# Forward scan of a hybrid trunk: output factors loaded one chunk ahead, through a ring of seven

## The chip, the cores and the metric

One kernel on one core of a Trainium2 chip. The metric is device time in microseconds of the whole launch; the median of the timed runs stands for a kernel. Engines: PE multiplies matrices (PEld is its weight load), DVE is the vector engine, ACT the scalar engine with its function tables, POOL the third elementwise engine, SP the queue from which nearly all transfers are issued.

## What is computed

Two layers, each with a normalised input, one input projection, four mixers and one output projection. The change lies in one mixer, a state-space scan that runs over the sequence in both directions in chunks. For one direction:

```python
cs = jnp.cumsum(da, axis=-1)                          # da = dt * a, per head
lmat = jnp.exp(jnp.where(lower, cs[..., :, None] - cs[..., None, :], -jnp.inf))
y_diag = einsum(cb[:, :, :, None] * lmat, xdt)        # inside a chunk
chunk_states = einsum(bc, exp(cs[..., -1:] - cs), xdt)
h = h * exp(cs[..., -1]) + chunk_states               # from chunk to chunk
y_off = einsum(cc, prev, jnp.exp(cs))                 # from the chunks before
y = y_fwd + y_bwd + d_skip * xh
y = rmsnorm(y * silu(z), norm_w)
```

`exp(cs)`, by which `y_off` is multiplied, is what the text calls the output factors.

## The kernel before

The sequence has 1040 positions, channels lie on partitions. Filler work, the output projections of the other mixers (`outproj`, three matmul passes, lines 132 to 134, 12 matmuls for one output tile, scalar copy L349 and POOL addition L350 or DVE addition L352 behind it), is woven into the scan by `weave`. The order in which the code is written gives priorities; a scheduler then fixes an order for each engine and gives each tile a free slot of its pool. Every engine works through its own order and waits where a row is not ready.

The backward scan `ssd_bwd` leaves one state for each chunk. The forward scan `ssd_fwd` goes over ten chunks of 104 positions (q = 0 to 9) in two parts:

- `prepare(q)` loads two copies of the cumulative sums, `rf` and `rb`, broadcast over the partitions, from `csd` (L865, L866), transposes the chunk (`ssd_tok`), and makes the decay matrix: eight times DVE L880 and ACT L881 on `rf`, masks L877 and L878, eight times ACT L884 and DVE L885 into `rb`, and one POOL product L886 of the two. `rf` is free after L886, `rb` after the matmuls L911.
- `finish(q, st)` loads the output factors `e` from `ecd` with two transfers (L894), multiplies the parts that come from the backward state (matmul L822, DVE L897) and from the forward state (L822, DVE L900) by them, makes the new state (`ssd_state`: DVE L805, matmul L808, POOL L814, DVE L815), adds the two parts on POOL (L905), runs the matmuls inside the chunk (L911), adds them (DVE L912) and writes four tiles of `y` (DVE L914).

The matmul L808 writes the accumulator tile that L900 reads, so L808 waits for L900. Where an output part of `CH` is complete (after chunks 3, 6 and 9), `ssd_fin` gates it with z (ACT table load and SiLU at L306, DVE L947), squares it (ACT L949, DVE L951), and in a second half sums over partitions (matmul L954), takes the reciprocal root (`rstd`: ACT L138 Ln, L140 Exp, L142, DVE L143 to L145) and scales (DVE L958). SiLU is in another table of ACT than Ln and Exp; L307 asks for the table that has both of these.

`rf` and `rb` come from the pool `bb`, which has 5 slots of 8 x 104 floats; `e` comes from the common pool `big`. The order of the parts is prepare 0, prepare 1, finish 0, prepare 2, finish 1, and so on; the second half of a norm is written behind the prepare that follows its first half.

## Time and profile before

| | us |
|---|---|
| median of 3 runs (lowest, highest) | 2119.06 (2115.15, 2121.02) |
| profiled execution | 2122.54 |
| its span in the trace | 2120.80 |
| PE, DVE, ACT, POOL busy | 1995.3, 1396.7, 1012.3, 461.1 |
| first and last L897 of layer 0 | 914.2, 1038.4 |
| first and last L897 of layer 1 | 1955.5, 2070.9 |

The profiled execution is 3.48 us above the median and 1.52 us above the slowest of the three runs; 1.74 us of it lie around its span. The trace gives, for each instruction, start, duration and, in brackets, how long its engine stood idle before it and on whom it waited. A group line gives the count, the busy time with the mean in ns, and the idle time before the group. Start times are microseconds from the start of the span.

### The profile page before, as it was taken

The page shows a single profiled execution, that of the slowest core. Times are in us where ns is not written, and L with a number is a line of the kernel's source. Part 1 is how long each engine was busy: PE and PEld are TensorE (multiplying, and loading weights), DVE is VectorE, ACT ScalarE, POOL GpSimd, SP SyncE. Part 2 cuts the span into 40 slices and gives each one's busy share as a digit, 9 for nine tenths or more (in the row PEclk, how much of TensorE's full clock was granted, in tenths as well). Part 3 has the DMA queues.
Part 4 walks back from the last instruction along what each step waited for, and adds up shares of the span by engine and source line. Part 5 has one row for each costly group of instructions (what it writes and reads, how often), then busy time and mean ns, then how long its engine had stood idle before and what let it go on. Part 6 is the DMA issues. An engine that isn't in the chain of part 4 may idle for free.

```text
span 2120.8 us, 33393 instructions
## 1 busy us (share of the span) xinstructions
PE 1995.3 (94%) x11880; PEld 1747.7 (82%) x11880; DVE 1396.7 (66%) x2781; ACT 1012.3 (48%) x2191; POOL 461.1 (22%) x465
## 2 busy tenths in 40 slices
PE   6999999999999998888899999999999999989888
PEld 4898988688899778877779988877888996878878
DVE  5575547767665555689786755477676636476996
ACT  5534344463543546356465343436534425563652
POOL 2012122022120300245220121221311203012550
PEclk8999999999999999999999999999999999999999
DMA  4321222122232567676643221122223335867766
GB/s 139 100 75 60 67 64 57 42 74 97 92 125 97 171 196 249 188 184 187 172 130 112 75 67 54 58 61 69 71 89 104 119 112 169 243 215 183 185 176 194
DMA packets 164669, 261.01 MB, mean 123 GB/s; under 512 B 20938, under 2 KB 113678, under 8 KB 164502
## 3 DMA queue, kind: packets, MB, share of 16 engines
q1 hardware_dynamic: 161846, 249.56, 39.3%
q0 software_dynamic: 2656, 9.33, 1.8%
q8 instruction: 93, 1.52, 0.3%
q14 instruction: 74, 0.61, 0.1%
HBM read 182.92 MB, written 71.67 MB: 120 GB/s over the span
## 4 chain that ended last, share of the span: by engine, by line
PE 66%; DVE 12%; DMA 10%; ACT 5%; issue 4%; POOL 3%; SPq 1%; DVEq 0%; POOLq 0%; ACTq 0%
PE psmm L132 10%; PE psmm L133 10%; PE psmm L134 10%; PE pspv L675 6%; PE psy L132 5%; PE psy L133 5%; PE psy L134 5%; PE psy L652 2%; PE psy L623 2%; DMA hd<-sms 2%; PE psy L653 2%; DMA big<-md 2%; DMA sms<-hd 2%; DMA sms<-md 1%; PE pssc L652 1%
## 5 line engine op out<-in xcount | busy, mean ns | idle before, releaser
L132 PE MATMUL psmm<-big,wh 128*128 128x346 f32 (+2 forms) x1920 | 643.5, 336 | 29.3 <-ACT sms L349 10.3
L133 PE MATMUL psmm<-big,wh 128*128 128x346 f32 (+2 forms) x1920 | 632.3, 329 | 6.0 <-DVE big L129 3.2
L134 PE MATMUL psmm<-big,wl 128*128 128x346 f32 (+2 forms) x1920 | 626.1, 326 | 1.3 <-DVE wl L129 1.3
L132 PEld LDWEIGHTS psmm<-big,wh 128*128 128x128 f32 x1920 | 369.6, 193 | 74.7 <-issue 29.2
L133 PEld LDWEIGHTS psmm<-big,wh 128*128 128x128 f32 x1920 | 369.3, 192 | 15.6 <-DVE big L129 5.4
L134 PEld LDWEIGHTS psmm<-big,wl 128*128 128x128 f32 x1920 | 369.2, 192 | 4.7 <-DVE wl L129 2.4
L665 POOL TENSOR_TENSOR acc<-acc,pf 116x346 f32<-116x346 f32 (+5 forms) x216 | 220.8, 1035 | 673.4 <-ACT pf L655 534.0
L128 ACT CAST wh<-wr 128x512 fp32r<-128x512 f32 (+1 forms) x236 | 145.1, 616 | 264.1 <-PE psmm L133 207.3
L129 DVE TENSOR_TENSOR wl<-wr,wh 128x512 fp32r<-128x512 f32 x232 | 170.1, 737 | 126.6 <-ACT wh L128 125.3
L132 PE MATMUL psy<-big,wh 128*128 128x346 f32 (+2 forms) x672 | 221.6, 330 | 1.0 <-ACT big L128 0.4
L133 PE MATMUL psy<-big,wh 128*128 128x346 f32 (+2 forms) x672 | 217.5, 324 | 2.6 <-DVE big L188 1.5
L134 PE MATMUL psy<-big,wl 128*128 128x346 f32 (+2 forms) x672 | 216.6, 322 | 0.0
L655 ACT ACTIVATE pf<-psy 116x346 f32<-116x346 f32 (+4 forms) x288 | 125.1, 456 | 90.2 <-PE psy L653 89.0
L675 PE MATMUL pspv<-pf,vt 116*64 116x346 f32 (+5 forms) x864 | 166.0, 465 | 0.0
L665 DVE TENSOR_TENSOR acc<-acc,pf 116x346 f32<-116x346 f32 (+5 forms) x120 | 108.8, 907 | 77.1 <-ACT pf L655 50.8
L624 DVE TENSOR_REDUCE mx<-psy 116x1 f32<-116x346 f32 (+3 forms) x272 | 132.8, 511 | 17.6 <-PE psy L623 17.1
L132 PEld LDWEIGHTS psy<-big,wh 128*128 128x128 f32 x672 | 126.9, 189 | 12.9 <-issue 7.4
L133 PEld LDWEIGHTS psy<-big,wh 128*128 128x128 f32 x672 | 126.8, 189 | 6.0 <-DVE big L188 2.3
L134 PEld LDWEIGHTS psy<-big,wl 128*128 128x128 f32 x672 | 127.0, 189 | 0.8
L675 PEld LDWEIGHTS pspv<-pf,vt 116*64 116x64 f32 (+1 forms) x864 | 59.0, 136 | 61.6 <-issue 25.8
L624 DVE TENSOR_REDUCE mx<-pssc 128x1 f32<-128x346 f32 (+3 forms) x136 | 69.9, 514 | 41.4 <-PE pssc L623 39.8
L652 PE MATMUL psy<-big,big 128*116 128x346 f32 (+4 forms) x288 | 95.5, 333 | 1.0 <-DVE mx L624 0.9
(292 smaller groups left out, 3310.7 us busy)
## 6 DMA issues: line engine op xcount, KB each, us to landing
wr<-w SPq DMA_DIRECT2D x248, 256.0 KB
sms<-hd SPq DMA_DIRECT2D x112, 173.0 KB
hd<-sms SPq DMA_DIRECT2D x96, 173.0 KB
bb<-csd SPq DMA_DIRECT2D x40, 338.0 KB
md<-big SPq DMA_DIRECT2D x24, 520.0 KB
gd<-sms SPq DMA_DIRECT2D x64, 173.0 KB
big<-gd SPq DMA_DIRECT2D x16, 520.0 KB
big<-md SPq DMA_DIRECT2D x16, 520.0 KB
```

What stands on the lines that cost most here:

```text
L128: nc.scalar.copy(hi, src)
L129: nc.vector.tensor_tensor(lo, src, f(hi), op=ALU.subtract)
L132: nc.tensor.matmul(out_ps, ah, bh, start=start, stop=False)
L133: nc.tensor.matmul(out_ps, ah, bl, start=False, stop=False)
L134: nc.tensor.matmul(out_ps, al, bh, start=False, stop=stop)
L623: nc.tensor.matmul(p[:qn, :cw], s1[e][:, q0:q0 + qn], k1[:, c0:c0 + cw], start=True, stop=True)
L624: nc.vector.tensor_reduce(mx[:qn, q, e, ci:ci + 1], p[:qn, :cw], axis=AX.X, op=ALU.max)
L652: nc.tensor.matmul(p[:n, :cw], k1[:, k0:k0 + n], s1[e][:, cs], start=True, stop=False)
L653: nc.tensor.matmul(p[:n, :cw], k3[0:65, k0:k0 + n], q2[e][0:65, cs], start=False, stop=True)
L655: nc.scalar.activation(pf[:n, :cw], p[:n, :cw], AF.Exp, scale=0.125)
L665: eng.tensor_tensor(accs[c0, e][:n, :cw], accs[c0, e][:n, :cw], pf[:n, :cw], op=ALU.add)
L675: nc.tensor.matmul(hold["pv"][64 * e:64 * e + 64, :cw], s.vt[:n, k, v, :], pfs[e][:n, :cw], start=(k == 0), stop=(k == len(KTS) - 1))
```

## The change

The output factors are loaded by a function of their own, `load_factors`, into the pool `bb`, which grows from 5 to 7 slots. The factors of chunk q + 1 are asked for at the end of step q, ahead of prepare q + 2, and those of chunk 0 behind prepare 0. The loop is written out anew: prepare 0, prepare 1, and then finish q and prepare q + 2 in turn, with as many steps between the weaves as before. The second half of a norm now stands behind the next finish instead of behind the prepare before it. The small tiles `bt` of the scan get 4 slots instead of 3.

```diff
--- before.py
+++ after.py
@@ -71,7 +71,7 @@
     epst = const.tile([128, 1], F32, name="epst")
     nc.vector.memset(epst, EPS)
     FW, TW = 17, 20
-    NBIG, NBB = 30, 5
+    NBIG, NBB = 30, 7
     WB = (4, 5)
     PB, KB, NPF, NACC = 2, 3, 14, 4
     SPARE = (('xx', 'xx', 'mm'), ('sc', 'sc', 'mm'), ('xx', 'mm', 'xx'), ('xx', 'sc', 'xx'))
@@ -886,12 +886,18 @@
             nc.gpsimd.tensor_tensor(rb, rb, rf, op=ALU.mult)
             ready[q] = (xt, xw, bt, rb)
 
+        factors = {}
+
+        def load_factors(q):
+
+            e = factors[q] = vr(bb())
+            for a in range(2):
+                nc.sync.dma_start(e[64 * a:64 * a + 64].rearrange("p (i j) t -> p i j t", i=2), s.ecd[q, :, 4 * a:4 * a + 4].partition_broadcast(64))
+
         def finish(q, st):
             qs = slice(q * QC, (q + 1) * QC)
             xt, xw, bt, rb = ready.pop(q)
-            e = vr(big())
-            for a in range(2):
-                nc.sync.dma_start(e[64 * a:64 * a + 64].rearrange("p (i j) t -> p i j t", i=2), s.ecd[q, :, 4 * a:4 * a + 4].partition_broadcast(64))
+            e = factors.pop(q)
             if q < NQ - 1:
                 pb = ssd_off(s, q, s.sb[q], "sc")
                 nc.vector.tensor_tensor(e[:, 4:8], pb.rearrange("p (j t) -> p j t", t=QC), e[:, 4:8], op=ALU.mult)
@@ -916,20 +922,25 @@
 
         s.sf = big()
         st = norm = None
-        for q in range(NQ + 1):
-            if q < NQ:
-                prepare(q)
+        prepare(0)
+        load_factors(0)
+        yield
+        prepare(1)
+        yield
+        for q in range(NQ):
+            st = finish(q, st)
             if norm is not None:
                 next(norm, None)
                 norm = None
-            if q < NQ:
-                yield
-            if q:
-                st = finish(q - 1, st)
-                ci = next((i for i, (c0, cw) in enumerate(CH) if (q - 1) * QC < c0 + cw <= q * QC), None)
-                if ci is not None:
-                    norm = ssd_fin(l, s, ci)
-                    next(norm)
+            ci = next((i for i, (c0, cw) in enumerate(CH) if q * QC < c0 + cw <= q * QC + QC), None)
+            if ci is not None:
+                norm = ssd_fin(l, s, ci)
+                next(norm)
+            if q + 1 < NQ:
+                load_factors(q + 1)
+            yield
+            if q + 2 < NQ:
+                prepare(q + 2)
                 yield
         next(norm, None)
         yield
@@ -1064,7 +1075,7 @@
         run(islice(fill2, 1))
         run(weave((tabs, 5), (main, 2.5), (islice(fill2, FB[2] - 1), FB[2] - 1)))
         scope.close()
-        phase["p"], phase["q"] = scope.enter_context(tc.tile_pool(name=nm("ssdp"), bufs=1)), 3
+        phase["p"], phase["q"] = scope.enter_context(tc.tile_pool(name=nm("ssdp"), bufs=1)), 4
         stage(fft_inner(l, s), 9, FB[1])
         outer = fft_outer(l, s)
         stage(islice(outer, OS[0]), OS[0], FB[3])
```

Below the change L880 to L886 keep their numbers; L894 becomes L895, L897 L903, L900 L906, L905 L911, L911 L917, L912 L918, L914 L920, and `ssd_fin` stands 11 lines further down (L947 is L958, L949 L960, L951 L962, L954 L965, L958 L969). The rows below are of layer 0.

The SP queue before, from the factors of chunk 0 (`big_9059`) over those of chunk 1 (`big_9217`) to those of chunk 2 (`big_9398`); `bb_9300` is `rb` of chunk 3, `bb_9474` and `bb_9475` are `rf` and `rb` of chunk 4; the other rows serve the filler:

```order
L894 DMA big_9059<-ecd_3642 64x2x416 x2
L353 DMA hd_5735<-sms_9200 128x346
L866 DMA bb_9300<-csd_3641 104x832
L894 DMA big_9217<-ecd_3642 64x2x416 x2
L865 DMA bb_9474<-csd_3641 104x832
L338 DMA sms_9280<-hd_5734 128x346
L866 DMA bb_9475<-csd_3641 104x832
L353 DMA hd_5730<-sms_9261 128x348
L338 DMA sms_9354<-hd_5735 128x346
L353 DMA hd_5731<-sms_9280 128x346
L894 DMA big_9398<-ecd_3642 64x2x416 x2
```

The SP queue now, where the factors of chunk 2 (`bb_9255`) are asked for; `bb_9132` is `rb` of chunk 2:

```order
L866 DMA bb_9132<-csd_3641 104x832
L338 DMA sms_8794<-hd_5728 128x346
L353 DMA hd_5734<-sms_8718 128x346
L353 DMA hd_5735<-sms_8735 128x346
L895 DMA bb_9255<-ecd_3642 64x2x416
L338 DMA sms_8831<-hd_5729 128x346
L353 DMA hd_5733<-sms_8777 128x348
L338 DMA sms_8857<-hd_5727 128x348
L895 DMA bb_9255<-ecd_3642 64x2x416
```

The factors of chunk 2 stood behind the sums of chunk 4, and stand now right behind the sums of chunk 2, some 30 rows earlier in the queue.

DVE before, at finish 3 (`big_9554` holds its factors, `big_8874` the state):

```order
L897 TENSOR_TENSOR big_9554<-pssc_9557,big_9554 128x416
L900 TENSOR_TENSOR big_9554<-pspv_9563,big_9554 128x416
L912 TENSOR_TENSOR big_9554<-big_9554,psxx_9578 128x416
L815 TENSOR_TENSOR big_8874<-big_8874,pspv_9571 128x512
L914 SCALAR_TENSOR_TENSOR big_8187<-big_8187,vecs,big_9554 128x104
L914 SCALAR_TENSOR_TENSOR big_8188<-big_8188,vecs,big_9554 128x104
```

The same place now (`bb_9436` holds the factors of chunk 3, `bb_9652` and `bb_9653` are `rf` and `rb` of chunk 5):

```order
L903 TENSOR_TENSOR bb_9436<-pssc_9557,bb_9436 128x416
L906 TENSOR_TENSOR bb_9436<-pspv_9563,bb_9436 128x416
L880 SCALAR_TENSOR_TENSOR bb_9652<-bb_9653,gap_8180,bb_9652 104x104 x3
L918 TENSOR_TENSOR bb_9436<-bb_9436,psxx_9578 128x416
L815 TENSOR_TENSOR big_8874<-big_8874,pspv_9571 128x512
L920 SCALAR_TENSOR_TENSOR big_8187<-big_8187,vecs,bb_9436 128x104
L920 SCALAR_TENSOR_TENSOR big_8188<-big_8188,vecs,bb_9436 128x104
```

Three L880 of a later chunk now stand between the multiplication by the factors and the addition of the matmul inside the chunk.

ACT before, at the first norm, second half (`smn_9706` to `smn_9710` are its tiles, `z_10157` is z of the second norm; L881 belongs to chunk 6, L349 to the filler):

```order
L138 ACTIVATE smn_9706<-psxx_9704,epst 128x348
L870 COPY big_9859<-psy_9849 104x512
L140 ACTIVATE smn_9708<-smn_9706 128x348
L881 ACTIVATE bb_9845<-bb_9845,big_8184 104x104
L142 ACTIVATE smn_9710<-smn_9708 128x348
L349 COPY sms_9740<-psmm_9727 128x348
L881 ACTIVATE bb_9845<-bb_9845,big_8184 104x104 x5
L349 COPY sms_9759<-psmm_9746 128x346
L306 ACT_TABLE_LOAD
L306 ACTIVATE z_10157<-z_10157 128x4x346
L349 COPY sms_9816<-psmm_9803 128x346
L307 ACT_TABLE_LOAD
```

ACT now, at the same norm (`smn_9788` to `smn_9792` are its tiles, `bb_9848` is `rf` of chunk 6):

```order
L306 ACT_TABLE_LOAD
L306 ACTIVATE z_10157<-z_10157 128x4x346
L349 COPY sms_9747<-psmm_9734 128x346
L138 ACT_TABLE_LOAD
L138 ACTIVATE smn_9788<-psy_9786,epst 128x348
L349 COPY sms_9819<-psmm_9806 128x346
L140 ACT_TABLE_LOAD
L140 ACTIVATE smn_9790<-smn_9788 128x348
L881 ACTIVATE bb_9848<-bb_9848,big_8184 104x104
L142 ACTIVATE smn_9792<-smn_9790 128x348
```

The SiLU of z of the next norm has moved ahead of the Ln of this one. Ln and Exp now have a table load each, and the load of L307 has moved behind the rows shown. Counted over the program, ACT has 69 table loads instead of 61: four more in each layer, at the first and the second norm.

DVE before, at the same norm (`big_9763` holds the factors of chunk 4):

```order
L900 TENSOR_TENSOR big_9763<-pspv_9772,big_9763 128x416
L880 SCALAR_TENSOR_TENSOR bb_9845<-bb_9846,gap_8180,bb_9845 104x104 x3
L143 SCALAR_TENSOR_TENSOR smn_9710<-psxx_9704,smn_9710 128x348
L880 SCALAR_TENSOR_TENSOR bb_9845<-bb_9846,gap_8180,bb_9845 104x104
L144 TENSOR_SCALAR smn_9710<-smn_9710 128x348
L815 TENSOR_TENSOR big_8874<-big_8874,pspv_9780 128x512
L145 TENSOR_TENSOR smn_9708<-smn_9708,smn_9710 128x348
L912 TENSOR_TENSOR big_9763<-big_9763,psy_9787 128x416
L958 SCALAR_TENSOR_TENSOR big_8187<-big_8187,vecs,smn_9708 128x348
```

DVE now (`bb_9611` holds the factors of chunk 4):

```order
L906 TENSOR_TENSOR bb_9611<-pspv_9757,bb_9611 128x416
L880 SCALAR_TENSOR_TENSOR bb_9848<-bb_9849,gap_8180,bb_9848 104x104 x3
L918 TENSOR_TENSOR bb_9611<-bb_9611,psxx_9772 128x416
L815 TENSOR_TENSOR big_8874<-big_8874,pspv_9765 128x512
L920 SCALAR_TENSOR_TENSOR big_8187<-big_8187,vecs,bb_9611 128x104
L920 SCALAR_TENSOR_TENSOR big_8188<-big_8188,vecs,bb_9611 128x104
L920 SCALAR_TENSOR_TENSOR big_8189<-big_8189,vecs,bb_9611 128x104
L920 SCALAR_TENSOR_TENSOR big_8190<-big_8190,vecs,bb_9611 128x104
L880 SCALAR_TENSOR_TENSOR bb_9848<-bb_9849,gap_8180,bb_9848 104x104 x2
L129 TENSOR_TENSOR wl_10275<-wr_10272,wh_10274 128x512
L143 SCALAR_TENSOR_TENSOR smn_9792<-psy_9786,smn_9792 128x348
```

The norm's L143 stood ahead of L815 and L912 of the chunk, and stands now behind all of this finish. From chunk 9 on, the rows of PE are the same in the last layer.

## Prediction

> **What bounds the kernel now.** I read the page's busy shares first, then a table by stage, then the waits inside the two scan stages, and last the rows around each wait that the change touches.
>
> ```profile
> PE 1995.3 (94%) x11880; PEld 1747.7 (82%) x11880; DVE 1396.7 (66%) x2781; ACT 1012.3 (48%) x2191; POOL 461.1 (22%) x465
> ```
>
> Over the whole launch PE is the bound. The change acts only in two scan stages, so the table by stage (start and end, length, busy time of each engine, granted clock, share of the DMA engines) decides:
>
> ```profile
> 914.00:1013.00 99.00, 83.58 (x586) 77.38 (x586) 90.33 (x215) 58.28 (x167) 52.48 (x47) 0.95 0.69 188
> 1955.00:2054.00 99.00, 86.18 (x601) 79.86 (x599) 91.52 (x216) 58.30 (x168) 53.41 (x47) 0.93 0.69 183
> 2090.00:2121.00 31.00, 23.68 (x146) 23.06 (x146) 16.53 (x34) 7.25 (x14) 0.00 (x0) 0.95 0.63 171
> ```
>
> In the steady part of both scans (99 us each) DVE is busy 90.33 and 91.52 us, PE only 83.58 and 86.18. DVE sets the pace there: it idles 8.7 and 7.5 us, PE 15.4 and 12.8 us. What PE waits for there, layer 0 first (total, times, longest):
>
> ```profile
> PE pspv L808 <- DVE big L900: 8.5, 6, 3.1
> PE psy L954 <- DVE sms L951: 8.2, 2, 6.1
> ...
> PE pspv L808 <- DVE big L900: 8.6, 4, 3.0
> PE psy L954 <- DVE sms L951: 4.9, 2, 3.0
> ```
>
> PE's largest wait is for L900, so for DVE in `finish`. What DVE itself waits for, by groups over the launch (busy and mean ns, then idle and releaser), is small:
>
> ```profile
> L880 DVE SCALAR_TENSOR_TENSOR bb<-bb,gap,bb 104x104 f32<-104x104 f32 x160 | 61.5, 435 | 7.8 <-DMA bb<-csd 7.7
> L897 DVE TENSOR_TENSOR big<-pssc,big 128x416 f32<-128x416 f32 x18 | 10.5, 585 | 5.4 <-DMA big<-ecd 5.2
> L912 DVE TENSOR_TENSOR big<-big,psxx 128x416 f32<-128x416 f32 x10 | 5.8, 584 | 6.3 <-POOL big L905 6.1
> L912 DVE TENSOR_TENSOR big<-big,psy 128x416 f32<-128x416 f32 x10 | 5.8, 577 | 2.9 <-POOL big L905 2.9
> ```
>
> The factors cost 5.2 us of DVE waiting in both layers together, POOL's addition L905 9.0 us. These are the two waits that the change can take. The order of prepare and finish is the same before and after, so the overlap of chunks is no gain.
>
> **Factors asked for earlier.** Forty transfers in both, so nothing is added on SP. The four places where DVE waited for them:
>
> ```profile
> 944.44 0.59 DVE L897 TENSOR_TENSOR big<-pssc,big 128x416 f32<-128x416 f32 x1 [0.77 <-DMA big<-ecd]
> 1038.36 0.59 DVE L897 TENSOR_TENSOR big<-pssc,big 128x416 f32<-128x416 f32 x1 [2.37 <-DMA big<-ecd]
> 1985.20 0.59 DVE L897 TENSOR_TENSOR big<-pssc,big 128x416 f32<-128x416 f32 x1 [0.84 <-DMA big<-ecd]
> 2033.37 0.59 DVE L897 TENSOR_TENSOR big<-pssc,big 128x416 f32<-128x416 f32 x1 [1.26 <-DMA big<-ecd]
> ```
>
> Sum 0.77 + 2.37 + 0.84 + 1.26 = 5.24. The factors now stand a chunk earlier in the SP queue. One steady chunk takes some 14 us (99 us for seven), and a transfer of factors on the chain of waits took
>
> ```profile
> 1005.96 3.91 DMA big<-ecd
> ```
>
> 3.91 us. All four waits go: **-5.2**. The ends are 0 (something else comes last at each place) and -12.4 (at each place a wait of PE for L900 as long as the longest above, 3.1, goes whole). I take the DVE figure, since DVE paces.
>
> **L880 ahead of L912.** Finish 3 now has three L880 between L900's row and L912's, as finish 2 and 4 had before. They would fill DVE's wait for POOL, 9.0 us. Rows with POOL idle and with POOL busy:
>
> ```profile
> 916.87 1.99 DVE L880 SCALAR_TENSOR_TENSOR bb<-bb,gap,bb 104x104 f32<-104x104 f32 x8 [0.17 <-DMA bb<-csd]
> 929.19 4.00 DVE L880 SCALAR_TENSOR_TENSOR bb<-bb,gap,bb 104x104 f32<-104x104 f32 x3
> ...
> 928.91 1.95 POOL L886 TENSOR_TENSOR bb<-bb,bb 104x832 f32<-104x832 f32 x1
> 930.82 1.08 POOL L905 TENSOR_TENSOR big<-big 128x416 f32<-128x416 f32 x1
> ```
>
> Eight took 1.99 us, 0.25 each; three took 4.00 us beside POOL's L886 and L905, and ended just after them (933.19 against 931.90). So L880 stood still while POOL worked. Filling the wait with it moves the wait into a longer L880. I take **0**; the ends are -9.0 (all of it) and +2.0 (a row that ends a little after POOL, as here by 1.3 us, once or twice).
>
> The Trainium skill (SBUF — State Buffer, section "Who interferes with whom") says that a vector instruction with two inputs in SBUF and a GpSimd instruction that reads SBUF exclude each other for a whole instruction, whichever started first. L880 has two such inputs, and the row of 4.00 us agrees. By that rule this term is 0; by the order of the rows alone it would be -9.0, and the sum -11.2 in place of -2.2.
>
> **Slots of `bb`.** Seven slots now hold the factors too. In the order of SP, `rb` of chunks 4 to 7 waits for DVE, that is for L914 of an earlier finish, where it waited for PE's L911. L912 starts once L911 is done, and L914 ends here:
>
> ```profile
> 947.41 0.59 DVE L912 TENSOR_TENSOR big<-big,psxx 128x416 f32<-128x416 f32 x1 [1.88 <-POOL big L905]
> 948.51 1.81 DVE L914 SCALAR_TENSOR_TENSOR big<-big,vecs,big 128x104 f32<-128x104 f32 x4
> ...
> 933.26 4.54 DMA bb<-csd
> 2010.89 6.20 DMA bb<-csd
> ...
> L885 DVE SCALAR_TENSOR_TENSOR bb<-cfb,big,bb 104x104 f32<-104x104 f32 x160 | 49.2, 366 | 1.2 <-ACT bb L884 1.2
> L129 DVE TENSOR_TENSOR wl<-wr,wh 128x512 fp32r<-128x512 f32 x232 | 170.1, 737 | 126.6 <-ACT wh L128 125.3
> L805 DVE TENSOR_TENSOR big<-big,big 104x256 f32<-104x256 f32 x36 | 17.8, 525 | 4.0 <-ACT big L870 4.0
> L877 DVE TENSOR_TENSOR cfb<-psy,ct 104x208 f32<-104x208 f32 x12 | 4.4, 365 | 0.0
> ```
>
> So the load may start 950.3 - 947.4 = 2.9 us later, and takes 4.5 to 6.2 us. The tightest place is chunk 5: between L914's end and its first L880 stand one L129, L877, its twin L878, two L805 and five L885, 0.74 + 2 x 0.37 + 2 x 0.53 + 5 x 0.37 = 4.4 us of DVE work; it would wait 0.1 to 1.8 us in each layer. The other chunks have more rows in between. I take 0.75 us a layer, **+1.5**; ends -7.7 (all the waits of L880 for `csd` go) and +7.2 (two chunks a layer at 1.8).
>
> **Table loads.** Eight more on ACT, four in each layer. Their price, and ACT at the first norm before:
>
> ```profile
> L306 ACT ACT_TABLE_LOAD x24 | 30.8, 1283 | 2.3 <-DMA big<-gd 1.2 <-DMA big<-md 0.8
> ...
> 956.13 0.53 ACT L138 ACTIVATE smn<-psxx,epst 128x348 f32<-128x348 f32 x1
> 957.03 0.51 ACT L140 ACTIVATE smn<-smn 128x348 f32<-128x348 f32 x1
> 957.69 0.49 ACT L142 ACTIVATE smn<-smn 128x348 f32<-128x348 f32 x1
> 962.27 0.43 ACT L349 COPY sms<-psmm 128x346 f32<-128x346 f32 x1
> 962.71 1.28 ACT L306 ACT_TABLE_LOAD   x1
> 964.01 1.36 ACT L306 ACTIVATE z<-z 128x1384 f32<-128x1384 f32 x1
> 967.05 0.45 ACT L349 COPY sms<-psmm 128x346 f32<-128x346 f32 x1 [1.68 <-POOL sms L350]
> ```
>
> 8 x 1.283 = 10.3 us of ACT, which is busy 58.28 of 99 us, so 5.1 us a layer fit into its 40.7 idle. But L143 on DVE waits for L142. From the first load to the end of L142 ACT now has 3 x 1.28 for loads, 1.36 for SiLU, 0.53 + 0.51 + 0.49 for Ln, Exp and square, two L349 (0.45) and one L881 (as the square, 0.49): 8.1 us, 9.8 with one wait of 1.68 for POOL and 11.5 with two. The load may begin ahead of the finish: its L881 is that of an L880 with three L885 (1.1 us) between it and L897, less the L881 itself, so 0.6 us ahead. On DVE finish 3 ran from L897 at 944.44 to L914's end at 950.3, 5.9 us, with a wait for POOL where three L880 stand now; two L880 (0.5) and one L129 (0.7) follow: 7.1 us to L143. The wait is 8.1 - 0.6 - 7.1 = 0.4 or 9.8 - 0.6 - 7.1 = 2.1 us, and 11.5 - 7.1 = 4.4 us if the load begins with L897 and both L349 wait. I take 1 us at each of the four norms, between the first two, less the one that stood there before:
>
> ```profile
> 1010.77 0.52 DVE L143 SCALAR_TENSOR_TENSOR smn<-psy,smn 128x346 f32<-128x346 f32 x1 [1.43 <-ACT smn L142]
> ```
>
> 4 - 1.4 = **+2.5**; ends -1.4 and +16.2 (4.4 four times, less 1.4).
>
> The Trainium skill (ScalarE: Activation LUTs, section "What ACT_TABLE_LOAD costs") gives 1283 ns for a load and adds a drain of about 1380 ns to each switch of the set. The load agrees; the drain does not show here: SiLU starts at 964.01, and 962.71 + 1.28 = 963.99. With the drain this term would grow by at most 8 x 1.38 = 11.0 us.
>
> **Norm behind the finish.** PE's L954 waited for L951 at the second norm, since it stood close behind it; now a whole prepare and finish lie between:
>
> ```profile
> 1004.46 0.82 PE L954 MATMUL psy<-sms,ones 128*128 128x346 f32 x2 [2.08 <-DVE sms L951]
> 2044.82 0.82 PE L954 MATMUL psy<-sms,ones 128*128 128x346 f32 x2 [1.92 <-DVE sms L951]
> ```
>
> 4.0 us of PE's slack; DVE's pace does not shorten by it. I take a quarter, **-1.0**; ends -4.0 and 0. The splits of the output tiles (L129) for the filler of chunk 8 come later by the same step, but two filler tiles stand ahead of them on PE. The third norm keeps its tables and its place, and the last stage (2090 to 2121) has the same rows: 0. The slots of `bt` and the loop as such issue nothing: 0.
>
> **Sum.** -5.2 + 0 + 1.5 + 2.5 - 1.0 = -2.2 us against the profiled execution of 2122.54, so 2120.3 there. That execution lay 3.5 us above the median of 2119.06; on the median's scale this is 2116.9, **2117 us**. The runs before spread over 2115.15 to 2121.02, 5.9 us or 0.28%, so 0.3% (6.4 us) is about what a measurement can tell from no change.
>
> **Rivals.** *Faster:* POOL's addition is really covered, since POOL is often done when L880 starts, and PE's waits for L900 shrink with it. For it: 9.0 us of such waits and 17.1 us of waits for L900. Against it: the row of 4.00 us. Its time: -5.2 - 9.0 + 1.5 + 2.5 - 1.0 = -11.2, 2108 us.
>
> *Slower:* the table loads put L143 late at each norm, with everything of the next chunk queued behind it on DVE. For it: the loads stand ahead of Ln and Exp, and DVE has no row to pass L143. Against it: ACT has 40 us of slack a stage, and 4.4 us needs both L349 late. At 4.4 us each the term is 16.2, the sum -5.2 + 1.5 + 16.2 - 1.0 = +11.5, 2131 us. It decides from (6.4 + 4.7 + 1.4) / 4 = 3.1 us a norm, 4.7 being what the other terms save.
>
> *No effect by another wait:* the factors are there, and L880's sums come last in their place (+7.2 instead of +1.5, sum +3.5): 2123 us. That counts as no change.
>
> The Trainium skill's drain, if it showed, would take the slower rival to 2142 us; the gap of 0.02 us before SiLU leaves that little chance.
>
> **Chances.** No measurable change, by the sum or with the wait exchanged: 0.52. Faster, mostly the rival with POOL covered: 0.27. Slower, mostly the table loads: 0.21. The range runs from the faster rival to short of the slower one, whose four norms would all have to be late: 2108 to 2128; the likeliest case alone has 2112.7 to 2125.4.
>
> **What would show it.** L903 without a wait for `ecd` proves the first step. The second is right if L918 waits less for POOL and the L880 in front of it are longer than 0.25 us by about as much; it is wrong if they stay short. L880's waits for `csd` above 7.7 us show the slots. L143's waits for L142 give the price of the loads; the steady parts then need 99 us less or more for the same seven chunks. The forecast fails if DVE's pace is not what ties the chunks together, so that PE's waits of 15 us a scan move by more than DVE's.

## The result, and the profile after

The changed kernel is slower: 2131.81 us (four runs, 2127.61 to 2134.68) against 2118.75 us for the kernel before on the same chip (2115.15 to 2121.02), a ratio of 1.0053 with a 95% interval of 1.0036 to 1.0071. That is 13 us more by the medians and 11 by the ratio, where 2117 was forecast with a range up to 2128. The profiled execution took 2132.95 us, its span 2131.2 us. First the page's busy shares:

```profile
PE 1995.2 (94%) x11880; PEld 1751.0 (82%) x11880; DVE 1396.1 (66%) x2781; ACT 1022.1 (48%) x2199; POOL 461.2 (22%) x465
```

PE is busy for the same 1995 us as before, and so is DVE. The 10.4 us by which the span grew are idle time of PE. What PE waits for, largest first (total, times, longest):

```profile
PE pspv L808 <- DVE bb L906: 24.9, 10, 5.1
PE psmm L132 <- DVE sms L352: 17.0, 12, 6.5
...
PE psy L965 <- DVE sms L962: 5.7, 2, 4.5
...
PE psxx L132 <- DVE big L129: 3.8, 1, 3.8
```

The same list of the kernel before:

```profile
PE pspv L808 <- DVE big L900: 17.2, 10, 3.1
PE psy L954 <- DVE sms L951: 13.1, 4, 6.1
...
PE psmm L132 <- DVE sms L352: 5.1, 4, 1.7
```

L808's wait grew by 7.7 us and the filler's wait for L352 by 11.9; the last kind, 3.8 us, is new; the norm's matmul waits 7.4 us less. The 3.8 us and the longest of the filler's waits, 6.5 us, do not lie in a scan. They lie in the Fourier stages ahead of the scans, which the prediction does not mention. Of the filler's other waits for L352, 10.2 us lie in the backward scans, where all 5.1 us of them lay before. The last L429 and the first L808 of layer 0 enclose the Fourier stage. Before:

```profile
758.50 1.02 PE L429 MATMUL psxx<-big,big 128*1 128x512 f32 x2
...
840.23 1.03 PE L808 MATMUL psy<-big,smq 104*128 104x256 f32 x4
```

and after:

```profile
757.25 1.02 PE L429 MATMUL psxx<-big,big 128*1 128x512 f32 x2
...
842.59 1.03 PE L808 MATMUL psy<-big,smq 104*128 104x256 f32 x4
```

81.7 us became 85.3, 3.6 more; in layer 1 the stage takes 4.7 us more (taken in the same way: 80.4 before, 85.1 after). The 3.6 us of layer 0 do not last. The last L429 of layer 1, with which its Fourier stage begins, and the first L822 of its forward scan, before:

```profile
1801.08 1.02 PE L429 MATMUL psxx<-big,big 128*1 128x512 f32 x2
...
1951.16 1.04 PE L822 MATMUL pssc<-big,big 128*128 128x104 f32 x8
```

and after:

```profile
1799.17 1.02 PE L429 MATMUL psxx<-big,big 128*1 128x512 f32 x2
...
1955.39 1.04 PE L822 MATMUL pssc<-big,big 128*128 128x104 f32 x8
```

When the Fourier stage of layer 1 begins, the changed kernel is 1.9 us ahead. All that this profile loses, it loses in layer 1: 4.7 us in the Fourier stage, 1.4 from there to the forward scan, 6.1 in the forward scan. SP's queue inside the Fourier stage of layer 0, before:

```profile
772.08 1.09 SPq L338 DMA_DIRECT2D sms<-xT  x2
773.22 0.43 SPq L942 DMA_DIRECT2D z<-gd  x1
775.30 2.99 SPq L353 DMA_DIRECT2D hd<-sms  x2
784.17 1.09 SPq L338 DMA_DIRECT2D sms<-xT  x2
```

and after:

```profile
771.96 0.40 SPq L866 DMA_DIRECT2D bb<-csd  x1
773.30 0.33 SPq L353 DMA_DIRECT2D hd<-sms  x1
773.67 0.63 SPq L895 DMA_DIRECT2D bb<-ecd  x1
775.67 0.33 SPq L353 DMA_DIRECT2D hd<-sms  x1
782.76 0.33 SPq L338 DMA_DIRECT2D sms<-xT  x1
783.15 0.59 SPq L895 DMA_DIRECT2D bb<-ecd  x1
...
785.38 0.44 SPq L865 DMA_DIRECT2D bb<-csd  x1
...
788.06 0.43 SPq L953 DMA_DIRECT2D z<-gd  x1
```

Seven free slots let seven early tiles into the queue 130 to 160 us before the forward scan, where five let five: the factors of chunk 1 (L895) and the sums of chunk 2 (L865) are asked for here, and z, that stood ahead of the pause of the queue at 776 us, is asked for 15 us later. ACT's next row is the SiLU of z. So in this profile ACT stands still, then DVE, then PE, here in layer 1 (start, duration, and in brackets the idle time before and its releaser):

```profile
1838.95 1.31 ACT L306 ACTIVATE z<-z 128x1328 f32<-128x1328 f32 x1 [9.28 <-DMA z<-gd]
```

```profile
1840.76 0.69 DVE L129 TENSOR_TENSOR big<-psxx,big 128x512 fp32r<-128x512 f32 x1 [11.67 <-ACT big L128]
```

```profile
1842.51 0.65 PE L132 MATMUL psmm<-big,wh 128*128 128x332 f32 x1 [6.53 <-DVE sms L352]
```

Inside the forward scans DVE waits for the sums. The group of L880 (count, busy, mean ns, then idle and releaser), and one of its waits with what follows on DVE and on PE:

```profile
L880 DVE SCALAR_TENSOR_TENSOR bb<-bb,gap,bb 104x104 f32<-104x104 f32 x160 | 68.3, 475 | 11.1 <-DMA bb<-csd 11.0
```

```profile
946.40 0.33 DVE L880 SCALAR_TENSOR_TENSOR bb<-bb,gap,bb 104x104 f32<-104x104 f32 x1 [2.32 <-DMA bb<-csd]
946.64 1.52 DVE L885 SCALAR_TENSOR_TENSOR bb<-cfb,big,bb 104x104 f32<-104x104 f32 x3
948.09 0.57 DVE L903 TENSOR_TENSOR bb<-pssc,bb 128x416 f32<-128x416 f32 x1
948.59 0.57 DVE L906 TENSOR_TENSOR bb<-pspv,bb 128x416 f32<-128x416 f32 x1
```

PE there, the matmul that needs L906's tile:

```profile
949.22 2.07 PE L808 MATMUL pspv<-big,smq 104*128 104x256 f32 x4 [5.08 <-DVE bb L906]
```

All seven such waits now lie in the two forward scans, 11.0 us; before, 7.7 us in all, of which 2.2 there. An L880 that waited over 2 us stands shortly ahead of L906 in three of L808's four longest waits (5.1, 4.8 and 4.1 us). L903 itself no longer waits for the factors.

### The profile page after: what moved, and what is told of

It reads as the page before. It is cut to its first block, busy times and chain, and to the rows that moved or that the text cites. A ratio compares the mean times of both kernels' runs of the same rounds, so it can differ in the third digit from the quotient of the medians.

```text
span 2131.2 us, 33388 instructions
## 1 busy us (share of the span) xinstructions
PE 1995.2 (94%) x11880; PEld 1751.0 (82%) x11880; DVE 1396.1 (66%) x2781; ACT 1022.1 (48%) x2199; POOL 461.2 (22%) x465
## 5 line engine op out<-in xcount | busy, mean ns | idle before, releaser
L624 DVE TENSOR_REDUCE mx<-psy 116x1 f32<-116x346 f32 (+3 forms) x272 | 132.7, 511 | 15.9 <-PE psy L623 15.3
L675 PEld LDWEIGHTS pspv<-pf,vt 116*64 116x64 f32 (+1 forms) x864 | 58.9, 136 | 61.5 <-issue 25.7
L352 DVE TENSOR_TENSOR sms<-sms,psmm 128x346 f32<-128x346 f32 (+2 forms) x104 | 52.6, 508 | 72.0 <-PE psmm L134 41.9
```

What stands on the lines that cost most here:

```text
L352: nc.vector.tensor_tensor(o, ht, p[:, :cw], op=ALU.add)
L624: nc.vector.tensor_reduce(mx[:qn, q, e, ci:ci + 1], p[:qn, :cw], axis=AX.X, op=ALU.max)
L675: nc.tensor.matmul(hold["pv"][64 * e:64 * e + 64, :cw], s.vt[:n, k, v, :], pfs[e][:n, :cw], start=(k == 0), stop=(k == len(KTS) - 1))
```

## The experiments

Five explanations were tried. A: the extra slots let loads into the Fourier stage, and these delay it. B: the sums come late inside the scans, for want of a slot or behind other rows of the queue. C: the norm's new place and its table loads. D: seven slots give another order inside the scans, which is slower. E: the larger pool in itself. "Fourier" in the table is how much longer the two Fourier stages together are than before, "last scan" the same for the last forward scan (from its first L822 to the last norm's matmul; 141.2 us before), both from one profile each; "L880" is its wait for the sums over the whole launch in that profile (7.7 before, of which 2.2 inside the forward scans). A profile is one execution. It lay above the median of its kernel by 3.5 us for the kernel before, 3.8 for e5, 4.7 for e9, 4.1 for e14 and 9.3 for e16, below it by 3.7 for e7, 5.4 for e10 and 7.6 for e6, and within 2.2 of it for the others of the table. The difference in time is between medians taken together on one chip, with the ratio's interval behind it.

| | us over before (95%) | Fourier | last scan | L880 |
|---|---|---|---|---|
| changed kernel | +13.1 (0.36 to 0.71%) | +8.3 | +6.1 | 11.0 |
| e1 z first | +17.8 (0.73 to 0.99%) | +8.9 | +10.6 | 11.9 |
| e2 norm back | +5.4 (0.14 to 0.40%) | +8.5 | +2.5 | 12.2 |
| e3 factors in `big`, 5 slots | +1.4 (-0.04 to 0.19%) | -0.8 | +2.7 | 1.8 |
| e4 before, 7 slots | +13.0 (0.47 to 0.83%) | +7.7 | -2.1 | 9.1 |
| e5 before, 7, two held | +13.1 (0.44 to 0.74%) | +1.4 | +0.1 | 9.3 |
| e6 changed, two held | +17.9 (0.68 to 0.97%) | +2.8 | +7.2 | 8.3 |
| e7 = e3, norm back | -0.2 (-0.13 to 0.12%) | -2.8 | +5.8 | 3.3 |
| e8 before, norm moved | +6.0 (0.18 to 0.40%) | -2.3 | -1.8 | 6.0 |
| e9 before, 7, two unused | +0.7 (-0.07 to 0.18%) | -0.6 | +0.2 | 5.0 |
| e10 before, 6 slots | +4.7 (0.16 to 0.60%) | +1.6 | +0.9 | 5.0 |
| e11 changed, 6 slots | +4.0 (0.14 to 0.40%) | -0.2 | +5.8 | 7.4 |
| e12 = e6, norm back | +3.4 (0.05 to 0.39%) | +2.3 | +4.1 | 11.6 |
| e13 before, 7 early, 5 later | +6.5 (0.10 to 0.39%) | +7.2 | +4.0 | 11.4 |
| e14 before, 4 slots | +9.2 (0.30 to 0.64%) | +2.3 | +4.8 | 2.5 |
| e15 changed, two rings | +17.1 (0.47 to 1.01%) | +7.8 | +10.4 | 9.5 |
| e16 = e7, 4 slots | +6.0 (0.17 to 0.46%) | +8.6 | +6.9 | 4.6 |

**Which part of the change costs.** The factors were put back into the common pool, still one chunk ahead:

```diff
-    NBIG, NBB = 30, 7
+    NBIG, NBB = 30, 5
...
-            e = factors[q] = vr(bb())
+            e = factors[q] = vr(big())
```

> The changed kernel, with the factors in the common pool again and 5 slots for the sums; they are still asked for one chunk ahead. The early queue is then that of the kernel before, z included. Theory A alone: ACT's wait for z is below 2 us, the time falls by 8 to 11 us to 2121 to 2124. Rival B (slots): L808's wait for L906 falls from 24.9 to about 17 us as well; with A it would be 2114 to 2118, with B alone 2123 to 2126 and ACT's wait for z would not matter. If neither holds, 2129 or more.

2122.60 us, within measurement of the kernel before (2121.21). L808's wait for L906 is 19.8 us and ACT's wait for z is 0.2. With the old place of the norm besides (`next(norm, None)` behind `prepare(q + 2)` instead of behind `finish`):

> Factors in the common pool, 5 slots, asked for one chunk ahead (the third experiment), with the second half of a norm back behind the prepare. Rival C (the norm's new place costs some 5 us, as the second experiment suggests, 2126.6 against 2131.8): 3 to 6 us less than the third experiment, 2116 to 2120, below the kernel before. My prediction's terms (loads +2.5, norm -1.0): 1.5 us less, 2121. If the second experiment's gain came from slots taken in another order: no change, 2122 to 2124.

2118.12 against 2118.35 us: no measurable difference from the kernel before, though DVE waits less, by the list of its waits:

```profile
DVE big L918 <- POOL big L911: 4.2, 3, 2.6
DVE bb L880 <- DMA bb<-csd: 3.3, 3, 2.7
...
DVE big L903 <- DMA big<-ecd: 0.7, 1, 0.7
```

21.9 us of these three waits before (9.0, 7.7 and 5.2) are 8.2 here, and the median is the same. The profile is of the fastest of twelve executions, 8.1 us shorter than the profiled one before, but not by its forward scans: the two together take 287.5 us in both kernels. DVE stands idle in them for 27.6 us instead of 34.7, and is busy for 259.9 instead of 252.7. Over the launch the 36 rows of L805 with both inputs in SBUF grew most, from 17.8 us to

```profile
L805 DVE TENSOR_TENSOR big<-big,big 104x256 f32<-104x256 f32 x36 | 24.2, 691 | 3.4 <-ACT big L870 3.4
```

and the longest of them, 2.41 us, ran beside POOL's L886, L911 and L350. So asking for the factors earlier is worth nothing by itself, and the loss comes with the slots and the norm. The norm's place alone, both ways:

> The changed kernel, with the second half of a norm written behind the prepare that follows its first half, as before the change; ACT has 61 table loads again. Theory A (z late behind the early factors and sums): those loads stand as in the changed kernel, ACT still waits some 19 us for z, the time stays within 3 us of 2132. Rival C (table loads and the new place of the norm cost what was lost): the time falls by 8 us or more, to 2124 or less. My prediction's terms (loads +2.5, norm -1.0) would make it 1.5 us less.

> The kernel before with nothing changed but the place of the second half of a norm, which is written behind the next finish (63 table loads, not 69). Rival C: 4 to 6 us slower than the kernel before, 2124 to 2127. The prediction's terms: the wait of PE for L951 at the second norm goes (-1.0) and the few loads cost below 1, so no change, 2119 to 2122.

In the changed kernel, putting the norm back took it to 2126.62 us, from 1.0053 to 1.0027 of the kernel before. In the kernel before, moving it cost 6.0 us (2124.30), with two table loads more. There PE's wait for the norm's sum falls from 8.2 us to none in layer 0, and others take its place (window from 914 to 1075 us):

```profile
PE pspv L808 <- DVE big L900: 12.1, 6, 5.8
PE psmm L132 <- DVE big L352: 6.7, 2, 5.8
```

against 8.5 us for L808 before. C holds in its sign: by the table the norm's new place costs 7.7 and 6.0 us in these two pairs (5.5 in the first by the ratios, whose intervals overlap), and 1.6 us from e7 to e3, where the intervals overlap as well. The same four kernels give the price of the slots together with the place of the factors: 11.7 us with the norm moved (e3 to the changed kernel), 5.6 with it back (e7 to e2).

**The slots.** The kernel before with 7 slots (`NBIG, NBB = 30, 7`) and nothing else:

> The kernel before, with 7 slots instead of 5 in the pool of the sums and nothing else. Two more loads of sums are asked for during the Fourier stage and stand ahead of z, which comes 5 rows later in SP's queue, behind the place where the queue stood still for 7 us in the changed kernel. Theory A: ACT waits 3 to 6 us for z in each layer, PE loses 1 to 3 us a layer, the time rises by 2 to 6 us over the kernel before, to 2121 to 2125, though the sums have more room. Rival B (room for the sums is what matters): L880's waits for them go, L808 waits less, the time falls by 2 to 6 us to 2113 to 2117.

2134.16 us: as slow as the changed kernel, with no factor in the ring. Two slots that no load can use, taken by `s.held = [bb() for _ in range(2)]` with a one-column POOL memset each and given back at the end of the scan, leave every engine's order as it was but for those rows and one neighbour of them on POOL:

> The kernel before with 7 slots in the pool of the sums, two of which are taken when the pool is opened and given back only at the end of the forward scan, so that no load ever uses them. Every engine's order is that of the kernel before, but for the four small POOL rows a layer. It asks if the size of the pool in itself (where the tiles behind it lie) costs anything. Theories A and D (the loads and the order that the slots allow): no change, 2117 to 2122. Rival E (the larger pool itself): as slow as the two kernels with seven usable slots, 2130 to 2134.

2121.39 against 2120.70 us. E falls: the cost is in what the slots let happen. With 6 slots:

> The kernel before with 6 slots: one more load of sums in the Fourier stage, with z behind it by two rows only, still ahead of the place where the queue stands still. Theory A: the two Fourier stages together are at most 3 us longer than before (5.7 and 2.0 us with seven slots). Theory D (the order inside the scans): the scans and what follows are as much longer as in the held kernel, so 2124 to 2130 in all; by A alone 2118 to 2123.

2125.42 us, between 5 and 7. The Fourier stages are only 1.6 us longer in the profile, but that is the fastest of ten executions (2120.03 us) and does not show where the 4.7 us of the median lie. With 6 slots in the changed kernel:

> The changed kernel with 6 slots. The factors of chunk 1 still stand in the Fourier stage with z right behind them, behind the place where the queue stands still. Theory A: the two Fourier stages are 4 to 8 us longer than before together, ACT waits for z 10 us or more in all; the time is 2125 to 2132. Theory of the prediction (fewer slots make the sums of later chunks later): L880's waits for the sums rise above 15 us and the time is above 2134.

2124.70 us, a little below what either expected. ACT still waited 9.6 us for z, and the Fourier stages were not longer, so a late z does not by itself lengthen them.

**Where the slots cost.** Two slots are held until the channels of the scans are loaded; in the changed kernel the same lines were added:

```diff
+        s.held = [bb() for _ in range(2)]
+        for t in s.held:
+            nc.gpsimd.memset(t[:, :1], 0.0)
...
+        for t in s.held:
+            nc.gpsimd.tensor_tensor(t[:, :1], t[:, :1], s.xbc[7][:, :1], op=ALU.add)
```

> The kernel before with 7 slots in the pool of the sums, of which two are held: POOL writes one column of each when the pool is opened, and frees them with one small addition each that needs the last channel tile loaded for the scans. The sixth and seventh load then stand behind the loads of the scans, not in the Fourier stage. Theory A (the cost of the slots is the loads that they let into the Fourier stage): the filler at the start of the backward scans is within 2 us of the kernel before (with 7 slots free it was 4.6 and 12.6 us late), ACT does not wait for z, and the time is that of the kernel before within 3 us, 2118 to 2124, against 2134 with the slots free. Rival D (seven slots change the order inside the scans for the worse): 2130 or more, with the loss behind the start of the scans.

> The changed kernel with two of its seven slots held in the same way until the channels of the scans are loaded. Only the second half of the factors of chunk 0 and the sums of chunk 1 stay in the Fourier stage; the factors of chunk 1 and the sums of chunk 2 come behind the loads of the scans. Theory A: ACT's wait for z falls from 19.0 us to below 3, the filler at the start of the backward scans is within 2 us of the kernel before in layer 0 (was 2.4 late) and its lateness there in layer 1 falls from 6.6 to what layer 0 left; the time falls by 7 to 11 us to 2121 to 2125. What is left over the kernel before is then the norm's place and L808's waits. Rival D: no change, 2129 or more.

The Fourier stages are mended in both profiles (+1.4 and +2.8 us in place of +7.7 and +8.3). The medians are not: 2131.45 and 2136.20 us. Where they lose is not seen: the profile of e6 is its fastest execution, 2128.58 us. The span of e5's is 12.7 us longer than before. Of these, 4.7 lie in the scans (4.0 in layer 0, 0.7 in layer 1), and 5.5 between the layers, in a stage with a stretch at half the clock (last section). Three of its six executions have a mean granted clock of 0.968 to 0.971; the other three, at 0.975 to 0.977, have 2128.79 us in the middle, 10 over the kernel before. L880's waits inside the forward scans are 2.6 us in e5 and 3.2 in e4, hardly more than the 2.2 before, so late sums are not what these two lose by. With the norm back as well:

> The changed kernel with two slots held until the channels of the scans are loaded, and the second half of a norm back behind the prepare. What is left of the change is the factors one chunk ahead in the pool of seven. Theory A with C (Fourier stage 8 us, norm 5 us): 2117 to 2121, the kernel before within what can be measured. Theory D (seven slots cost in the scans whatever the Fourier stage does): 2126 to 2132, with the last layer's forward scan more than 4 us longer than before.

2124.05 us, between what A with C and what D expected. Here the norm's place is worth 14.5 us (17.9 to 3.4): its price depends on the order around it. The opposite of e5 has the early loads and only five slots from chunk 4 on (the two are taken behind `prepare(3)`):

> The kernel before with 7 slots until the sums of chunk 3 are asked for; from then on two are held to the end of the forward scan, and five are left. The Fourier stages have the same early loads as with seven slots (z behind them), the scans the five slots of before. Theory A (early loads): the two Fourier stages are 5 to 9 us longer together, the time 2124 to 2129. Theory D (only what the slots do inside the scans): the early loads are hidden in the end, 2118 to 2122. With seven slots throughout it was 13 us over the kernel before, with the early loads held back 13 as well.

2126.33 us, +6.5, with the Fourier stages 7.2 us longer: early loads with only five slots afterwards cost time in the median. That they cost it in the Fourier stages (A) is not shown: in the profile of e13 the first L822 of the last forward scan stands at 1951.40 us, 0.2 behind the kernel before, and 4.0 of the 4.6 us by which its span is longer are lost in that scan. And in e5 the slots cost 13 us without the early loads, in e4 13 us with them; by the medians the two costs do not add.

Is it z in the Fourier stage? Its load was moved to the head:

```diff
+        s.z0 = z_load(s, 0)
         prepare(0)
         load_factors(0)
...
```

> The changed kernel, with one edit: the load of z for the first norm is written ahead of prepare 0, so it stands first in SP's queue and not behind the early factors and sums. Theory A (the seven slots let the first factors and sums into the queue during the Fourier stage; z comes behind them, and ACT stands 9.7 us before its SiLU in each layer): ACT's wait for z falls from 19.0 us to below 2, PE is back at its old pace at the start of the backward scans (+2.4 and +2.8 us become about -1 and -2), the time falls by 8 to 11 us to 2121 to 2124. Rival B (the sums of the cumulative decay come late for want of slots, so that L808 waits 24.9 us instead of 17.2): no slot is changed here, the time stays at 2129 to 2135. Rival C (eight table loads more): the same, 2129 to 2135.

2139.03 us; the Fourier stages are as long as in the changed kernel, and ACT still waits for z though it is asked for first:

```profile
ACT L306 <- DMA z<-gd: 10.9, 2, 5.5
```

ACT's SiLU has moved ahead with the load, and both waits end as the Fourier stages begin (755.7 and 1800.0 us). So the stages are as long with no wait for z inside them, and in e11 they are not longer with one: the place of z is not the cause, and what lengthens them stays open. In the six kernels with all seven early tiles (changed, e1, e2, e4, e13, e15) the Fourier stages are 7.2 to 8.9 us longer; in the others of the table from -2.8 to +2.8, but for e16, whose profile of 2135.13 us was the slowest of its twelve runs.

**Inside the scans.** Rings of their own for sums (5) and factors (2):

```diff
-    NBIG, NBB = 30, 7
+    NBIG, NBB = 30, 5
...
-            e = factors[q] = vr(bb())
+            e = factors[q] = vr(phase["p"].tile([128, 8 * QC], F32, name=nm("ee"), tag="ee", bufs=2))
```

> The changed kernel with two rings in place of one: five slots for the sums, as before, and two for the factors. The same seven loads stand in the Fourier stage, with z behind them. Slots theory (the sums wait for a slot that the last reader of the factors frees): inside the scans L880's waits for the sums fall from 11.0 to below 4 us, L808's waits for L906 from 24.9 to below 20, the last forward scan loses at least half of its 6.1 us; the time is 2124 to 2128, with the Fourier stages still 6 to 10 us longer than before. If the shared ring does not matter: 2130 to 2134.

2136.87 us. L808 waits less (14.7 us), L880 nearly as much (9.5 us), the time is not better. So B's slots are not it: in this order the sums are late without sharing. In the queue of the changed kernel the loads behind the 2.32, 2.72 and 2.23 us waits each stand right behind a store of the filler; the last of them:

```profile
2037.09 0.32 SPq L353 DMA_DIRECT2D hd<-sms  x1
2037.51 0.35 SPq L866 DMA_DIRECT2D bb<-csd  x1
```

Issuing them from POOL (`nc.gpsimd.dma_start` in L865 and L866) was to settle it:

> The changed kernel with the loads of the sums issued by POOL and not by SP; slots and order as they are. Queue theory (the sums come late because they stand behind the filler's stores in SP's queue): L880's waits for them fall from 11.0 to below 5 us, L808's waits for L906 from 24.9 to below 20, the time falls by 3 to 8 us to 2124 to 2129; what is left is the norm's place and the early loads. Slots theory (they wait for the slot): the waits stay at 9 us or more and the time at 2130 to 2136. Against both: POOL issues the loads in its own order, behind its products, and may be later than SP; then the waits rise and the time is above 2136.

2154.67 us, 31.5 more than before. POOL issues them behind its own rows, and the waits grew:

```profile
L880 DVE SCALAR_TENSOR_TENSOR bb<-bb,gap,bb 104x104 f32<-104x104 f32 x160 | 74.6, 513 | 24.1 <-DMA bb<-csd 24.0
```

This says nothing for or against SP's queue.

**Tries for a better version.** Fewer slots, and e7 with POOL's queue:

> The kernel before with 4 slots: one load of sums less in the Fourier stage, z ten rows earlier in the queue. If less crowding there goes on paying (5, 6 and 7 slots gave 0, +0.4 and +0.6 per cent): 2113 to 2118. If the sums are then late in the scans, L880's waits for them rise from 7.7 us to above 15, and L808's with them: 2124 or more.

> Factors in the common pool and asked for one chunk ahead, the norm as before (the seventh experiment, 2118.1, no different from the kernel before), and 4 slots for the sums. A try for a version that beats both. By less crowding in the Fourier stage: 2110 to 2115. If four slots make the sums late in the scans: above 2121, with L880's waits for them above 10 us (3.3 with five).

> The seventh experiment (factors in the common pool one chunk ahead, norm as before, five slots; 2118.1) with the sums issued by POOL. A second try for a version that beats both kernels. Queue theory: the 3.3 us of waits for the sums go and SP's queue is shorter for the rest, 2112 to 2117. Otherwise 2118 to 2124.

2129.01, 2125.81 and 2152.44 us. With four slots L880's waits are small (2.5 and 4.6 us, not the late sums expected), and the kernels are slower all the same; PE waits 15.9 and 16.4 us for the filler's L349 (10.3 before). Why was not followed further. Five slots is the best number tried, and no version beats the kernel before.

## Why the prediction was wrong

- **Factors asked for earlier, -5.2.** The wait went as forecast: L903 waits for nothing in the group lines. It was worth nothing in time: e7 has this step without the slots and the norm's place, and measures -0.2 us, within -0.13 to 0.12%. That DVE's waits count in full, since DVE paces the scan, was the wrong part: 13.7 us of waits went in e7, and DVE's rows became 8.1 us longer in all (busy 1404.8 us against 1396.7), 6.4 of them in L805 beside POOL's rows. The prediction had this exchange for L880, and did not ask it of the rows that move up when a wait goes. Its doubt, that PE's waits might move by more than DVE's, is not what e7 shows: in the forward scans PE's idle time fell by 3.2 us (41.7 to 38.5), DVE's by 7.1. Its list of PE's waits covers the whole scans, not the 99 us: from 914 to 1013 PE waited 7.2 us for L900, 2.1 for L951, and 6.0 for the filler's L349, which the list leaves out.
- **L880 ahead of L912, 0.** There was no gain, as forecast, but the sign that was named for it, a shorter wait of L918, did not come: L918 waits 9.5 us for POOL (9.0 before), and L880 became longer by 6.8 us (68.3 against 61.5) beside POOL's rows. The Trainium skill's rule (SBUF — State Buffer, section "Who interferes with whom"), that the two exclude each other for whole instructions, is borne out by the trace here; by the order alone it would have been -9.0. Beside the row of 4.00 us POOL was at work for longer than the two rows shown there: its next one, an L350, ran from 931.86 to 932.82.
- **Slots of `bb`, +1.5 with an upper end of +7.2: the step that failed.** The slots cost 13.0 us in the kernel before (e4), 0.7 if nothing can use them (e9), and the changed kernel without them is 1.4 us over (e3), not 13.1. The prediction counted only when a slot comes free inside the scan, and only at chunk 5. First, it did not ask where the first loads of two more slots go; "nothing is added on SP" is true of their number, not of their place. They went into the Fourier stages, which are 8.3 us longer in the profile, though 3.6 of these were made good in layer 0; the kernel before with early loads and only five slots afterwards is 6.5 us slower in the median (e13). Second, "the other chunks have more rows in between" is wrong: waits of 0.25 to 2.72 us stand at seven places, 8.8 us more inside the forward scans than before.
- **Table loads, +2.5.** Their size was right as a wait of DVE; what they cost in time was not measured apart from the norm's place. L143's waits at the four norms are

```profile
974.26 0.52 DVE L143 SCALAR_TENSOR_TENSOR smn<-psy,smn 128x348 f32<-128x348 f32 x1 [1.78 <-ACT smn L142]
...
1025.11 0.51 DVE L143 SCALAR_TENSOR_TENSOR smn<-psy,smn 128x346 f32<-128x346 f32 x1
...
2018.08 0.50 DVE L143 SCALAR_TENSOR_TENSOR smn<-psy,smn 128x332 f32<-128x332 f32 x1 [1.75 <-ACT smn L142]
```

  and none at 2069.94; 1.78 + 1.75 - 1.43 = 2.1 us.
- **Norm behind the finish, -1.0.** Wrong sign. PE's waits of 2.08 and 1.92 us did go, but the place of the norm, with its table loads, costs 1.6, 7.7, 6.0 and 14.5 us in four pairs of kernels; the 6.0 comes with two table loads more, not eight.
- **The sum.** In the prediction's own terms the medians give -0.2 for the factors (e7), +1.6 for the norm and its tables at five slots (e3 less e7), and +11.7 for the slots (changed kernel less e3), where -5.2, +1.5 and +1.5 were forecast. The terms are not independent: at seven slots the norm's place costs more.
- **The rivals.** The slower one named 2131 us, and 2132 came, but by luck and other rows: L143's waits grew by 2.1 us, not 16.2. "No effect by another wait" had the right wait, that the sums come last in place of the factors, with 7.2 us at most. The faster rival fell: POOL's addition is not covered.

What stays open: by what way the slots cost. By the medians the early loads alone cost 6.5 us, seven slots without them 13, and both together 13, and no profile places these sums: e13 had made good its Fourier stages by the last forward scan, and e5 shows 4.7 us in the scans. Why the sums come late in the changed kernels with seven slots, whether the factors share their ring (11.0 us) or not (9.5), and with five in one ring do not (1.8), was not settled; that the order of the queue does it is only argued.

## What to carry to other kernels

More buffers in a pool also move its first loads forward, to where the pool opens: look in the order of the queue at what stage they land in, and what stands behind them there; then look whether a delay there still stands at the end of the layer. Try the number of slots alone, apart from the use meant for it, and a slot held unused, to tell the pool's size from what it lets happen. A wait that vanishes on one engine (21.9 to 8.2 us on DVE here) is no gain if its rows come to stand beside those of another engine that holds them up, and take as much longer (L805: 17.8 to 24.2 us). Compare the profiled execution with its median before reading a stage from it.

## What was not expected of the hardware

A wait of PE is followed by matmuls at half the clock. Stretches of the changed kernel, one that holds the wait of 5.08 us (944.1 to 949.2) and the one behind it (start and end, length, busy times, granted clock, DMA share, GB/s):

```profile
942.00:949.00 7.00, 2.14 (x24) 1.62 (x23) 4.68 (x12) 2.54 (x9) 2.60 (x3) 0.99 0.66 197
949.00:956.00 7.00, 6.78 (x22) 6.43 (x23) 7.00 (x14) 1.88 (x6) 3.45 (x4) 0.52 0.58 176
```

The granted clock falls from 0.99 to 0.52. Behind the waits of 3.76 and 6.53 us in the Fourier stages it was 0.53 and 0.63. The Trainium skill (TensorE: Matmul & The Clock Gate, "Part 1: The HAM clock gate") has half the clock after an idle window of some 3.4 us, and these three waits agree. But shorter ones were followed by half the clock too: behind the wait of 1.60 us that ends at 982.62 it was 0.51 from 983.0 to 986.4. So a wait costs more than itself: the four L808 behind the 5.08 us took 2.07 us, the four at 842.59, shown above, 1.03.

A second thing has no such wait ahead of it. In four of the 20 profiles (e3, e5, e9, e16) the clock was at one half for 20.5 us near 1430 to 1440 us, in a stage that no kernel here changes; in e9:

```profile
1420.00:1430.00 10.00, 9.47 (x43) 4.80 (x43) 9.17 (x27) 1.23 (x4) 0.00 (x0) 1.00 0.06 17
1430.00:1440.00 10.00, 9.64 (x24) 4.86 (x25) 5.43 (x15) 3.26 (x8) 1.99 (x3) 0.54 0.06 16
1440.00:1450.00 10.00, 9.96 (x25) 5.13 (x24) 8.91 (x27) 4.93 (x15) 3.02 (x3) 0.50 0.04 9
```

PE executed 24 and 25 matmuls there in 10 us, and 36 and 44 in the kernel before in the same stretches. Between 1416 and 1505 us e3 lost 5.6 us against the kernel before (its filler was 5.9 us ahead at the first and 0.3 at the second). One profile can so be several us off its median. In e9, whose order is that of the kernel before, the two Fourier stages are 2.1 us shorter and 1.4 us longer; differences of this size between single profiles say little.
